# Seven-product stage of a two-layer mixer trunk: running sums in other banks, convolution taps and rotary tables later, SiLU as one activation

## The chip, the cores and the metric

One NeuronCore of a Trainium2 chip runs the whole program in one launch. The metric is the device time of one execution in microseconds, taken as the median of several executions. The profile is one execution, recorded by the hardware.

## What is computed

The reference is a trunk of two layers over 512 tokens of width 1024. Each layer normalises its input and projects it with one wide weight matrix. The columns of the projection feed three groups of heads: a gated linear recurrence (RG-LRU, behind a causal convolution of width 4), a chunked retention with rotary positions, and a spatial gating unit (SGU). Each group is multiplied with a SiLU gate of its own, the results are joined and projected back, and a gated per-layer embedding is added.

```python
y = rms_norm(h, mix_norm[i])
x_lru, g_lru, q, k, v, g_ret, u_sgu, v_sgu, g_sgu = jnp.split(y @ w_in[i], split_points, axis=-1)
lru_out = rg_lru(causal_depthwise_conv(x_lru, ...), ...)     # sigmoid, exp, sqrt, scan
ret_out = retention(q, k, v, positions, ret_norm[i])         # rope on q and k
sgu_out = spatial_gating(u_sgu, v_sgu, ...)                  # LayerNorm of v, then mix
mixed = concatenate([lru_out * silu(g_lru), ret_out * silu(g_ret), sgu_out * silu(g_sgu)])
h = h + mixed @ w_out[i]
h = h + sigmoid(rms_norm(h, ple_norm[i]) @ w_ple_gate[i]) * (p[i] @ w_ple_proj[i])
```

## The kernel before, in words

Every matrix product is made of three TensorE matmuls (`mm3`, lines 217 to 221): each operand is split into a rounded high part and a remainder, and high by high, remainder by high and high by remainder are summed in PSUM. Activations lie transposed, 128 features by 512 tokens. Weights come in chunks of 128 by 1024 through `prefetch`: the load (`emit_raw`), then the split (`emit_cv`), high part on ScalarE (line 173) and remainder on VectorE (line 178). The order of the chunks is written out in `plan`; the split of a chunk is asked for four chunks before its use.

The work is a list of steps. `step` first asks for weights, then issues the step's matmuls, then takes up to three entries of the background queue `bg` (plain functions that issue small work), then the step's eviction, which reads PSUM. Python issues everything in that order, but the order on each engine is settled when the program is built; instructions may pass others that wait.

Of a layer's steps the first ones matter here. The six chunks of the recurrence's input are projected (`feat_steps` with `conv`, lines 531 to 547). `conv` evicts a PSUM bank with one multiplication (line 536), starts the convolution on ScalarE (line 537), adds three taps on VectorE (line 539) and writes the result into `U` by DMAs issued from ScalarE's queue (line 541). Then come seven products (`FAST`, `fast_step`, lines 574 to 606) that replace eight block products of the columns `v` and `v_sgu` after Strassen's scheme; `fast_sums` (lines 494 to 513) forms the sums of activations that five of them need, and is spread over the steps of the convolution by `bg`. Each product is 24 matmuls of 512 columns, two token tiles of 12. They add into three running sums X, Y and Z, each of two PSUM banks. Of the four banks with the tag `mm`, two hold X from the first product (W11) to the last; the other two hold Z for the second product (W21) and then Y for the third (Ta). Z is released by line 593, which adds it to `v`. Four of the seven weight operands are themselves running sums: the tile `rawq` of each half receives W11's block, and further blocks are added onto it in place by DMAs issued from GpSimd's queue (line 148), each one after the split of the sum before it: W11, then Ta, then Tc, then Td.

The order of the products is W11, W21, Ta, Tc, Tb, W22, Td. W22 adds onto Y, which Tb's eviction (lines 597 and 598) has to have read. In layer 0, `bg` holds the nineteen entries of `rope_tables` (lines 406 to 441) during the products. It uses four tiles of the pools with the tags `m2`, `r0` and `r1`. `ln_apply` (the LayerNorm of the SGU) and `bias_rows` are put into `bg` ahead of the last product.

After the products come the SGU's steps: four times a `u` step, whose matmuls end with `mix` (line 698, it reads the normalised `vs`), and a `gs` step, whose eviction is `silu_scaled` (lines 384 to 391); `lru_group` with four short gate steps stands before the second and the fourth pair; `sgu_out`, two more `lru_group` and the six heads of retention follow. The heads need the rotary tables.

Of the kernel before, what the change touches and what calls it, by code (L numbers as in the profile page):

```python
# [10 lines left out]
F32 = mybir.dt.float32  # L11
F32R = mybir.dt.float32r
I32 = mybir.dt.int32
AF = mybir.ActivationFunctionType
ALU = mybir.AluOpType

P = 128
DM, S, DEPTH = 1024, 512, 2
# [8 lines left out]
LRU_GROUPS = [(0, 1), (2, 3), (4, 5), (6, 7)]  # L27


FAST = (("W11", "x11", "X"), ("W21", "x12", "Z"), ("Ta", "u1", "Y"), ("Tc", "v2", "X"), ("Tb", "v3", "X"), ("W22", "u4", "Y"), ("Td", "x22", "X"))  # L30
FIRST = ("W11", "W21", "Ta")
RSQRT_MAGIC = 1597463007.0
ROUND = 12582912.0
# [2 lines left out]
LOOK = 4  # L36
# [58 lines left out]
def trunk(ctx, tc, a):  # L95
# [3 lines left out]
    tp = ctx.enter_context(tc.tile_pool(name="tp", bufs=2))  # L99
    ps = ctx.enter_context(tc.tile_pool(name="ps", bufs=4, space=bass.MemoryType.PSUM))  # L100
    V, SC, G, T = nc.vector, nc.scalar, nc.gpsimd, nc.tensor
# [4 lines left out]
    def slot_tiles(slots, name):  # L106
        return [cp.tile([P, S], F32, tag=f"a{s}", name=f"{name}{i}") for i, s in enumerate(slots)]

    def act_tiles(slots, name):

        t = [cp.tile([P, S], F32R, tag=f"a{s}", name=f"{name}{i}") for i, s in enumerate(slots)]
        return list(zip(t[0::2], t[1::2]))
# [3 lines left out]
    at, offs = 0, {}  # L116
# [77 lines left out]


    bg = deque()
    side = []

    def step(pe, evict=None, look=LOOK, n_bg=3, pre=None):
        prefetch(st["use"] + look)  # L200
        pe()
        for e in side:
            e[0] -= 1
        while side and side[0][0] <= 0:
            side.pop(0)[1]()
        for _ in range(min(n_bg, len(bg))):
            bg.popleft()()
        if pre:
            pre()
        if evict:  # L210
            evict()

    def drain():
        while bg:
            bg.popleft()()
# [7 lines left out]
    def bank(tag="mm", bufs=4, shape=(P, S), name="acc"):  # L223
        return ps.tile(list(shape), F32, tag=tag, name=name, bufs=bufs)
# [54 lines left out]
    nrm = {}  # L279
# [61 lines left out]
        nrm["rn"] = rn  # L341


    def feat_steps(l, y, kinds, evicts, look=LOOK, n_bg=3, mid=None):

        accs = []

        def pe():
            ws = [take(l, *k) for k in kinds]
            for _ in kinds:  # L350
                accs.append(bank())
            for k in range(KD):
                for acc, (wh, wl) in zip(accs, ws):
                    mm3(acc, wh[:, P * k : P * k + P], wl[:, P * k : P * k + P], *y[k], k == 0, k == KD - 1)
            if mid:
                mid()

        step(pe, lambda: [e(acc) for e, acc in zip(evicts, accs)], look=look, n_bg=n_bg)

    def tok_steps(l, y, off, evict):  # L360

# [22 lines left out]
    def silu_scaled(acc, name):  # L384

        x = tp.tile([P, S], F32, tag="sg", name=f"sx{name}", bufs=3)
        V.tensor_mul(x, acc, nrm["R"])
        g = tp.tile([P, S], F32, tag="sgm", name=f"sg{name}", bufs=1)
        SC.activation(g, x, AF.Sigmoid)
        V.tensor_mul(x, x, g)  # L390
        return x


# [10 lines left out]
        return out  # L404

    def rope_tables():
        ang = tp.tile([P, S], F32, tag="m2", name="ang")
        n1 = tp.tile([P, S], F32, tag="r0", name="n1")
        n2 = tp.tile([P, S], F32, tag="r1", name="n2")
        big = 2 * np.pi * 2.0**14  # L410
        c1 = parts(big, 9, 5)
        c2 = parts(2 * np.pi, 9, 5)

        tmp = tp.tile([P, S], F32, tag="m2", name="angt")
        p2 = float(np.float32(2 * np.pi))

        def red(n, c, out=ang, x=ang):
            return lambda: V.scalar_tensor_tensor(out, n, -c, x, op0=ALU.mult, op1=ALU.add)

        def first():  # L420
            V.tensor_copy(ang, posi)
            V.tensor_scalar(ang, ang, inv[:, 0:1], None, op0=ALU.mult)

        def rnd(n, m, x=ang):
            def f():
                V.tensor_scalar(n, x, float(1.0 / m), ROUND, op0=ALU.mult, op1=ALU.add)
                V.tensor_scalar(n, n, -ROUND, None, op0=ALU.add)

            return f

        def last():
            V.tensor_scalar(ang, ang, float(np.float32(3.1415925)), -float(np.float32(3.1415925)), op0=ALU.min, op1=ALU.max)
            SC.activation(sinT, ang, AF.Sin, scale=inv[:, 1:2])
            SC.activation(n1, ang, AF.Abs)
            SC.activation(cosT, n1, AF.Sin, scale=-1.0, bias=cst[:, 0:1])

        ops = [first, rnd(n1, big), red(n1, c1[0]), red(n1, c1[1])]
        ops += [red(n1, c1[2], out=tmp), red(n1, c1[3], out=tmp, x=tmp), rnd(n2, 2 * np.pi, x=tmp), red(n2, c2[0])]
        ops += [red(n1, c1[2]), red(n2, c2[1]), red(n1, c1[3]), red(n2, c2[2]), red(n1, c1[4]), red(n2, c2[3]), red(n2, c2[4])]
        ops += [rnd(n1, 2 * np.pi), red(n1, p2), red(n1, 2 * np.pi - p2), last]  # L440
        return ops
# [25 lines left out]
    y = act_tiles(SLOTS[0]["y"], "y0_")  # L467
# [9 lines left out]
    for l in range(DEPTH):  # L477
# [45 lines left out]
        def blocks(c):  # L523

            at = P * c
            while at < P * c + P:
# [2 lines left out]
                yield b, r, at - P * c, n  # L529
                at += n  # L530

        def conv(c):
            def f(acc):
                u = tp.tile([P, S], F32, tag="r1", name=f"xcv{c}")
                xs = tp.tile([P, S], F32, tag="sg", name=f"xs{c}", bufs=3)
                V.tensor_mul(xs, acc, nrm["R"])  # L536
                SC.activation(u, xs, AF.Identity, scale=col(V_CW, l * 24 + 18 + c), bias=col(V_CB, l * 6 + c))
                for j in range(1, 4):
                    V.scalar_tensor_tensor(u[:, j:], xs[:, : S - j], col(V_CW, l * 24 + 6 * (3 - j) + c), u[:, j:], op0=ALU.mult, op1=ALU.add)  # L539
                for b, r, r0, n in blocks(c):  # L540
                    nc.scalar.dma_start(out=U[r : r + n, b, :], in_=u[r0 : r0 + n, :])
            return f

        feat_steps(l, y, [("in", 0), ("in", P)], [conv(0), conv(1)], mid=norm_finish)
        bg.extend([f for j in range(4) for f in fast_sums(j)])
        for c in range(2, 6):
            feat_steps(l, y, [("in", P * c)], [conv(c)])
            if l == 0 and c == 2:
                softplus()
        rn = nrm["rn"]  # L550
# [10 lines left out]
        vs = slot_tiles(SLOTS[l]["vs"], f"vs{l}_")  # L561
# [8 lines left out]
        banks = {}  # L570

        def fast_step(name, xn, at):

            first = name in FIRST

            def pe():
                ws = [take(l, "fast", (name, c)) for c in range(2)]
                if first:
                    banks[at] = [bank() for _ in range(2)]
                for t in range(2):  # L580
                    for k in range(4):
                        wh, wl = ws[k // 2]
                        c = slice(512 * (k % 2), 512 * (k % 2) + 512)
                        xh, xl = fast_operand(xn, k, t)
                        mm3(banks[at][t], xh, xl, wh[:, c], wl[:, c], first and k == 0, k == 3, more=not first)

            def ev():
                for t in range(2):
                    acc = banks[at][t]
                    if name == "W11":  # L590
                        SC.copy(v4[t], acc)
                    elif name == "W21":
                        V.tensor_add(v4[t], acc, v4[t])  # L593
                    elif name == "Tc":
                        SC.copy(vs[t], acc)
                    elif name == "Tb":
                        SC.copy(vs[2 + t], acc)
                        V.tensor_sub(vs[2 + t], banks["Y"][t], vs[2 + t])
                        ln_stats(2 + t)
                    elif name == "W22":  # L600
                        V.tensor_sub(vs[t], acc, vs[t])
                        ln_stats(t)
                    elif name == "Td":
                        SC.copy(v4[2 + t], acc)

            step(pe, ev, n_bg=3)

        def ln_apply():
            for t in range(4):
                V.bn_aggr(mv[:, t, :], bst[:, t, :, :])  # L610
            vv = tp.tile([P, 4], F32, tag="nv", name="lnv")
            V.tensor_mul(vv, mv[:, :, 1], rn[:, 4:8])
            V.tensor_scalar(vv, vv, EPS, None, op0=ALU.add)
            r = rsqrt(vv, 4)
            V.tensor_mul(r, r, rn[:, 0:4])
            for t in range(4):
                V.tensor_scalar(vs[t], vs[t], mv[:, t, 0:1], r[:, t : t + 1], op0=ALU.subtract, op1=ALU.mult)
# [61 lines left out]
            bg.extend([tanh_exp, sqrts] + [recur(b) for b in grp])  # L679

        drain()
        if l == 0:
            bg.extend(rope_tables())
        for product in FAST[:-1]:
            fast_step(*product)
        bg.extend([ln_apply, bias_rows])
        fast_step(*FAST[-1])
        drain()


        sm = act_tiles(SLOTS[l]["sgu"], f"sm{l}_")
# [65 lines left out]
        sgu_out()  # L757
        drain()
        lru_group(3)
        rm = act_tiles(SLOTS[l]["ret"], f"rm{l}_")  # L760

        def values(h, n):
# [273 lines left out]
```

## Time and profile before

| | |
|---|---|
| median of 3 runs (lowest to highest) | 937.47 us (935.71 to 939.49) |
| the profiled execution's own time | 936.13 us |
| its span | 934.4 us |
| PE (TensorE matmul) busy | 905.3 us, 97% |
| DVE (VectorE) busy | 679.7 us, 73% |
| ACT (ScalarE) busy | 445.2 us, 48% |
| POOL (GpSimd) busy | 61.1 us, 7% |
| mean granted TensorE clock | 0.993 |

PE counts matmuls, PEld weight loads. A matmul is shown from its start to its modelled end, 0.39 us for 512 columns, while the next one starts some 0.23 us after it; a stall is read from the starts. The granted clock is a share of 2.4 GHz; a stretch at 0.5 ran at 1.2 GHz.

### The profile page before, as it was taken

The page shows a single profiled execution, that of the slowest core. Times are in us where ns is not written, and L with a number is a line of the kernel's source. Part 1 is how long each engine was busy: PE and PEld are TensorE (multiplying, and loading weights), DVE is VectorE, ACT ScalarE, POOL GpSimd, SP SyncE. Part 2 cuts the span into 40 slices and gives each one's busy share as a digit, 9 for nine tenths or more (in the row PEclk, how much of TensorE's full clock was granted, in tenths as well). Part 3 has the DMA queues.
Part 4 walks back from the last instruction along what each step waited for, and adds up shares of the span by engine and source line. Part 5 has one row for each costly group of instructions (what it writes and reads, how often), then busy time and mean ns, then how long its engine had stood idle before and what let it go on. Part 6 is the DMA issues. An engine that isn't in the chain of part 4 may idle for free. (4 is left out here: it accounts for less than half of the span.)

```text
span 934.4 us, 11725 instructions
## 1 busy us (share of the span) xinstructions
PE 905.3 (97%) x4354; PEld 751.3 (80%) x4354; DVE 679.7 (73%) x1310; ACT 445.2 (48%) x650; POOL 61.1 (7%) x57
## 2 busy tenths in 40 slices
PE   8969999999999999999999899999999999999997
PEld 5747887788898888888877688877889888888886
DVE  7998798897757784456649788889786767534564
ACT  6644566853232343343556446767333334434353
POOL 3210000000000000110321100000000000011020
PEclk9999999999999999999999999999999999999999
DMA  8876422332223233342586843222322324333302
GB/s 288 220 167 166 130 78 78 107 98 90 71 87 100 83 117 101 112 142 68 138 180 142 183 137 91 79 90 91 113 68 68 108 73 113 96 102 118 113 1 90
DMA packets 35034, 105.14 MB, mean 113 GB/s; under 512 B 4641, under 2 KB 5665, under 8 KB 34977
## 3 DMA queue, kind: packets, MB, share of 16 engines
q1 hardware_dynamic: 27536, 85.42, 28.6%
q0 software_dynamic: 3456, 12.58, 7.5%
q10 hardware_dynamic: 3984, 6.38, 2.3%
q8 instruction: 34, 0.56, 0.2%
q14 instruction: 24, 0.19, 0.1%
HBM read 95.99 MB, written 2.10 MB: 105 GB/s over the span
## 5 line engine op out<-in xcount | busy, mean ns | idle before, releaser
L173 ACT CAST whi<-raw 128x1024 fp32r<-128x1024 f32 (+2 forms) x158 | 154.3, 978 | 285.6 <-PE acc L220 210.4
L219 PE MATMUL acc<-y,whi 128*128 128x512 f32 x608 | 241.6, 397 | 0.5 <-DVE whi L171 0.4
L220 PE MATMUL acc<-y,whi 128*128 128x512 f32 x608 | 237.5, 391 | 2.5 <-DVE y L286 2.4
L221 PE MATMUL acc<-y,wlo 128*128 128x512 f32 x608 | 237.8, 391 | 1.0 <-DMA wlo<-in_wall 0.6
L178 DVE TENSOR_TENSOR wlo<-raw,whi 128x1024 fp32r<-128x1024 f32 (+3 forms) x154 | 172.6, 1123 | 77.9 <-ACT whi L173 77.3
L220 PEld LDWEIGHTS acc<-y,whi 128*128 128x128 f32 x608 | 114.4, 188 | 27.0 <-DVE y L286 4.5
L221 PEld LDWEIGHTS acc<-y,wlo 128*128 128x128 f32 x608 | 114.1, 188 | 26.3 <-DVE wlo L178 1.3
L219 PEld LDWEIGHTS acc<-y,whi 128*128 128x128 f32 x608 | 114.3, 188 | 24.0 <-DVE whi L171 0.6
L302 POOL TENSOR_TENSOR nacc<-nacc,sq 128x512 f32<-128x512 f32 (+1 forms) x26 | 36.5, 1403 | 496.2 <-ACT sq L292 495.9
L219 PE MATMUL acc<-z,whi 128*128 128x512 f32 (+1 forms) x144 | 53.0, 368 | 0.0
L221 PE MATMUL acc<-z,wlo 128*128 128x512 f32 (+1 forms) x144 | 52.8, 366 | 0.0
L220 PE MATMUL acc<-z,whi 128*128 128x512 f32 (+1 forms) x144 | 52.7, 366 | 0.0
L220 PE MATMUL acc<-wlo,y 128*128 128x256 f32 (+1 forms) x112 | 37.5, 335 | 2.8 <-DVE wlo L178 2.8
L219 PE MATMUL acc<-whi,y 128*128 128x256 f32 (+1 forms) x112 | 37.3, 334 | 1.8 <-DVE xs L536 1.8
L219 PE MATMUL acc<-whi,uy 128*128 128x512 f32 x64 | 27.5, 429 | 10.4 <-DVE v L593 8.1
L221 PE MATMUL acc<-rm,wlo 128*128 128x512 f32 x96 | 37.4, 389 | 0.0
L219 PE MATMUL acc<-ml,whi 128*128 128x512 f32 x96 | 37.4, 389 | 0.0
L220 PE MATMUL acc<-ml,whi 128*128 128x512 f32 x96 | 37.3, 389 | 0.0
L219 PE MATMUL acc<-rm,whi 128*128 128x512 f32 x96 | 37.3, 389 | 0.0
L220 PE MATMUL acc<-rm,whi 128*128 128x512 f32 x96 | 37.3, 389 | 0.0
L221 PE MATMUL acc<-ml,wlo 128*128 128x512 f32 x96 | 37.3, 389 | 0.0
L221 PE MATMUL acc<-whi,y 128*128 128x256 f32 (+1 forms) x112 | 36.8, 329 | 0.0
(236 smaller groups left out, 1640.6 us busy)
## 6 DMA issues: line engine op xcount, KB each, us to landing
raw<-in_wall SPq DMA_DIRECT2D x120, 512.0 KB, 3.5
raw<-in_wall SPq DMA_DIRECT2D x32, 384.0 KB, 3.0
rawq<-in_wall POOLq DMA_DIRECT2D x12, 512.0 KB, 5.5
wlo<-in_wall POOLq DMA_DIRECT2D x8, 512.0 KB, 8.6
hT<-in_xT SPq DMA_DIRECT2D x8, 256.0 KB, 5.9
rawq<-in_wall SPq DMA_DIRECT2D x4, 512.0 KB, 6.1
raw<-in_wall POOLq DMA_DIRECT2D x4, 512.0 KB, 7.2
out_dram<-o SPq DMA_DIRECT2D x8, 256.0 KB, 2.1
```

The source lines that it names most:

```text
L173: SC.copy(hi[:m, c], r[:m, c])
L178: V.tensor_sub(lo[:m, c], r[:m, c], f32(hi[:m, c]))
L219: T.matmul(out, wh, xh, start=first, stop=False, skip_group_check=more)
L220: T.matmul(out, wh, xl, start=False, stop=False, skip_group_check=more)
L221: T.matmul(out, wl, xh, start=False, stop=last, skip_group_check=more)
L302: (V if d == KD - 1 else G).tensor_add(nrm["acc"][:, c], nrm["acc"][:, c], sq[:, :n])
```

## The change

The order of the last two products is exchanged: Td now precedes W22. Z takes the two banks with the tag `sc` in place of two of the four `mm` banks. A second queue, `lazy`, gives one entry per step after those of `bg`. `conv` now multiplies the evicted bank into a tile that stays (`xs_at`), and puts the rest (start, three taps, DMAs) into `lazy`; the steps of chunks 2 to 5 take nothing from it, so that the six entries go with the first six products. `rope_tables` uses four long-lived tiles and goes into `lazy` after the seven products of layer 0; what is left of it is issued before the heads. `ln_apply` is issued directly after the seven products, `bias_rows` before them. `silu_scaled` calls one Silu activation in place of a Sigmoid and a multiplication.

```diff
-FAST = (("W11", "x11", "X"), ("W21", "x12", "Z"), ("Ta", "u1", "Y"), ("Tc", "v2", "X"), ("Tb", "v3", "X"), ("W22", "u4", "Y"), ("Td", "x22", "X"))
+FAST = (("W11", "x11", "X"), ("W21", "x12", "Z"), ("Ta", "u1", "Y"), ("Tc", "v2", "X"), ("Tb", "v3", "X"), ("Td", "x22", "X"), ("W22", "u4", "Y"))
...
-    def step(pe, evict=None, look=LOOK, n_bg=3, pre=None):
+    def step(pe, evict=None, look=LOOK, n_bg=3, pre=None, n_lazy=1):
...
+        for _ in range(min(n_lazy, len(lazy))):
+            lazy.popleft()()
...
         V.tensor_mul(x, acc, nrm["R"])
-        g = tp.tile([P, S], F32, tag="sgm", name=f"sg{name}", bufs=1)
-        SC.activation(g, x, AF.Sigmoid)
-        V.tensor_mul(x, x, g)
+        SC.activation(x, x, AF.Silu)
...
-        ang = tp.tile([P, S], F32, tag="m2", name="ang")
-        n1 = tp.tile([P, S], F32, tag="r0", name="n1")
-        n2 = tp.tile([P, S], F32, tag="r1", name="n2")
+        ang, n1, n2, tmp = slot_tiles((20, 21, 30, 31), "rope")
...
-        tmp = tp.tile([P, S], F32, tag="m2", name="angt")
...
+        xs_at = slot_tiles([*SLOTS[l]["vs"], *SLOTS[l]["v"][2:]], f"xs{l}_")
+
         def conv(c):
-            def f(acc):
+            xs = xs_at[c]
+
+            def taps():
                 u = tp.tile([P, S], F32, tag="r1", name=f"xcv{c}")
-                xs = tp.tile([P, S], F32, tag="sg", name=f"xs{c}", bufs=3)
-                V.tensor_mul(xs, acc, nrm["R"])
                 SC.activation(u, xs, AF.Identity, ...)
                 for j in range(1, 4):
                     V.scalar_tensor_tensor(u[:, j:], xs[:, : S - j], ...)
                 for b, r, r0, n in blocks(c):
                     nc.scalar.dma_start(out=U[r : r + n, b, :], in_=u[r0 : r0 + n, :])
+
+            def f(acc):
+                V.tensor_mul(xs, acc, nrm["R"])
+                lazy.append(taps)
...
-            feat_steps(l, y, [("in", P * c)], [conv(c)])
+            feat_steps(l, y, [("in", P * c)], [conv(c)], n_lazy=0)
...
-                    banks[at] = [bank() for _ in range(2)]
+                    banks[at] = [bank("sc", 2) if at == "Z" else bank() for _ in range(2)]
...
+        bg.append(bias_rows)
+        for product in FAST:
+            fast_step(*product)
+        ln_apply()
         if l == 0:
-            bg.extend(rope_tables())
-        for product in FAST[:-1]:
-            fast_step(*product)
-        bg.extend([ln_apply, bias_rows])
-        fast_step(*FAST[-1])
-        drain()
+            lazy.extend(rope_tables())
...
         lru_group(3)
+        while lazy:
+            lazy.popleft()()
```

## Rows read from the trace of the kernel before

**Rows 1.** The page, part 1: busy time of each engine.

```profile
PE 905.3 (97%) x4354; PEld 751.3 (80%) x4354; DVE 679.7 (73%) x1310; ACT 445.2 (48%) x650; POOL 61.1 (7%) x57
```

**Rows 2.** Stretches: length, busy us per engine, granted clock, DMA share, GB/s.

```profile
46.80:100.30 53.50, 43.99 (x171) 33.81 (x170) 49.81 (x86) 24.85 (x33) 4.32 (x5) 0.94 0.67 163
504.80:551.80 47.00, 41.49 (x170) 32.32 (x169) 39.81 (x69) 25.25 (x33) 4.31 (x5) 0.96 0.62 151
...
67.30:71.00 3.70, 3.70 (x10) 2.93 (x11) 2.50 (x5) 0.43 (x1) 0.03 (x1) 0.55 1.03 188
...
87.70:91.20 3.50, 3.48 (x8) 2.82 (x9) 3.50 (x6) 0.00 (x0) 0.00 (x0) 0.51 0.47 149
...
523.30:528.00 4.70, 4.70 (x14) 3.70 (x15) 2.24 (x6) 1.04 (x1) 0.00 (x0) 0.64 1.04 214
...
100.30:165.00 64.70, 64.11 (x298) 52.36 (x297) 54.20 (x89) 42.17 (x57) 0.00 (x0) 1.00 0.29 88
...
112.00:125.00 13.00, 13.00 (x63) 10.50 (x62) 9.76 (x15) 12.82 (x17) 0.00 (x0) 1.00 0.29 82
```

**Rows 3.** Timeline of PE, layer 0: start, us, instruction, idle before and its releaser.

```profile
53.16 1.02 PE L621 MATMUL rs<-ws,ones 128*128 128x512 f32 x2
...
67.29 0.76 PE L219 MATMUL acc<-whi,uy 128*128 128x512 f32 x1 [5.04 <-DVE v L593]
...
84.83 0.39 PE L220 MATMUL acc<-wlo,uy 128*128 128x512 f32 x1
85.06 0.39 PE L221 MATMUL acc<-whi,uy 128*128 128x512 f32 x1
87.72 0.80 PE L219 MATMUL acc<-whi,uy 128*128 128x512 f32 x1 [2.27 <-DVE vs L598]
```

**Rows 4.** Waits of PE, whole span: us in total, times, longest.

```profile
PE acc L219 <- DVE v L593: 8.1, 2, 5.0
PE acc L220 <- DVE wlo L178: 2.8, 4, 1.3
...
PE acc L219 <- DVE xs L536: 1.8, 3, 0.8
```

**Rows 5.** Timeline of DVE, layer 0, while PE waits for the third product.

```profile
62.26 0.73 DVE L539 SCALAR_TENSOR_TENSOR xcv<-xs,vec,xcv 128x509 f32<-128x509 f32 x1
...
64.39 0.41 DVE L427 TENSOR_SCALAR n<-n 128x512 f32<-128x512 f32 x1
64.73 1.21 DVE L178 TENSOR_TENSOR wlo<-rawq,whi 128x1024 fp32r<-128x1024 f32 x1
...
66.47 0.67 DVE L593 TENSOR_TENSOR v<-acc,v 128x512 f32<-128x512 f32 x1
```

**Rows 6.** Timelines of POOL, ACT and DVE: the next sum of the same weight tile.

```profile
66.46 0.86 POOL L148 DMA_DIRECT2D rawq<-in_wall  x1 [0.61 <-issue]
...
73.11 1.05 ACT L173 CAST whi<-rawq 128x1024 fp32r<-128x1024 f32 x1 [1.49 <-DMA rawq<-in_wall]
...
74.19 1.23 DVE L178 TENSOR_TENSOR wlo<-rawq,whi 128x1024 fp32r<-128x1024 f32 x1 [1.32 <-ACT whi L173]
```

**Rows 7.** Groups of DVE instructions by line and form: busy us, mean ns, idle before.

```profile
L418 DVE SCALAR_TENSOR_TENSOR ang<-n,ang 128x512 f32<-128x512 f32 x12 | 8.2, 681 | 0.1
L390 DVE TENSOR_TENSOR sxr<-sxr,sgr 128x512 f32<-128x512 f32 x12 | 8.2, 681 | 0.0
```

**Rows 8.** Timeline of ACT around the first group of recurrence gates, layer 0.

```profile
115.03 0.62 ACT L389 ACTIVATE sgs<-sxs 128x512 f32<-128x512 f32 x1
...
120.08 1.28 ACT L661 ACT_TABLE_LOAD   x1
121.38 1.34 ACT L661 ACTIVATE rg<-rg,spm 96x512 f32<-96x512 f32 x2
```

**Rows 9.** Timeline of DVE, layer 1: LayerNorm after the sixth product (W22).

```profile
547.96 0.68 DVE L601 TENSOR_TENSOR vs<-acc,vs 128x512 f32<-128x512 f32 x1
...
553.63 1.92 DVE L617 TENSOR_SCALAR vs<-vs,mv,rs_y 128x512 f32<-128x512 f32 x4
```

More of the change, by code (lines that the diff above doesn't have):

```diff
@@ L196, in trunk @@
     bg = deque()
+    lazy = deque()
     side = []
-    def step(pe, evict=None, look=LOOK, n_bg=3, pre=None):
+    def step(pe, evict=None, look=LOOK, n_bg=3, pre=None, n_lazy=1):
         prefetch(st["use"] + look)
@@ L341, in norm_bcast, with feat_steps @@
         nrm["rn"] = rn
-    def feat_steps(l, y, kinds, evicts, look=LOOK, n_bg=3, mid=None):
+    def feat_steps(l, y, kinds, evicts, look=LOOK, n_bg=3, mid=None, n_lazy=1):
         accs = []
@@ L356, in pe @@
                 mid()
-        step(pe, lambda: [e(acc) for e, acc in zip(evicts, accs)], look=look, n_bg=n_bg)
+        step(pe, lambda: [e(acc) for e, acc in zip(evicts, accs)], look=look, n_bg=n_bg, n_lazy=n_lazy)
     def tok_steps(l, y, off, evict):
@@ L604, in ev @@
                         SC.copy(v4[2 + t], acc)
-            step(pe, ev, n_bg=3)
+            step(pe, ev)
         def ln_apply():
```

## The prediction

> **What bounds the kernel now.** I read the engines' shares first. TensorE is busy for 97% of the span [rows 1], so apart from a shorter matmul stream, which this change does not bring, only its stalls and its slow clock can be won. The waits of TensorE name what it stalls on: VectorE, and above all line 593 and the splits of weights [rows 4]. The stretches then say where: the seven products take 53.50 us in layer 0 and 47.00 in layer 1 [rows 2]. What would they take without a stall? Two matmuls start 0.23 us apart [rows 3]; seven products of 24 matmuls are 168, so 38.6 us, and the product for `bias_rows` adds 1.0 [rows 3]: 39.6. Layer 0 thus loses 13.9 us and layer 1 7.4, together 21.3. That is the most that this stage can give.
>
> The timeline shows two kinds of loss. The third product (Ta) waits 5.04 us in layer 0 for line 593, and the sixth (W22) 2.27 us for line 598 [rows 3]; line 593 costs 8.1 us in two waits [rows 4], so 3.1 in layer 1. Behind each wait the clock is low: 0.55, 0.51 and 0.64 of 2.4 GHz over 3.70, 3.50 and 4.70 us [rows 2], so partly or wholly at 1.2 GHz after TensorE had stood still. Each costs its length times the missing share: 1.7 us three times.
>
> VectorE is why the waits are long. It is busy 49.81 of the 53.50 us [rows 2], and in the wait itself it does a convolution tap (62.26), a rotary operation (64.39) and the split of Ta's own second weight half (64.73) before line 593 at 66.47 [rows 5].
>
> **The change, part by part.**
>
> *Banks of Z.* Y gets free banks, since the convolution's banks that it takes over are long read. Line 593 no longer stands before Ta: 5.04 + 1.7 in layer 0, 3.1 + 1.7 in layer 1, 11.5 in all. A condition is that Ta's weights are there, and its split ended only at 65.9 [rows 5], 3.7 us after W21's last matmul. So the bank alone would win little; the relief of VectorE has to come with it.
>
> *Taps and rotary tables.* All 18 taps of layer 0, some 0.73 us each [rows 5], were issued ahead of Ta; now some two stages of three are due before it. The rotary tables leave altogether: 14 operations of 0.68 us [rows 7] and nine of some 0.41 [rows 5], 13.2 us. So VectorE is ahead by over 10 us where Ta's split is due, and that split's input was ready earlier. I take the whole 11.5. The waits for splits and banks inside the first two products are 2.8 + 1.8 [rows 4]; with the stumbles after them they are what is left of the 21.3, that is 5.8 after the 4.0 of the next part. Of these I take half, 2.9: a split also waits for its load.
>
> *Td before W22.* W22 no longer follows the eviction of Tb that it needs; 24 matmuls, 5.5 us, lie between, and the wait was 2.3. That gives 2.27 + 1.7 = 4.0, in layer 0 alone. Td adds onto X, whose copy by ScalarE has 12 matmuls of cover, as for Tb before. Td's loads on POOL's queue move up too, but they start when Tc's split ends, as now; W22's, on SP's, follow without need.
>
> *What the taps do in their new place.* They and their DMAs sit on ScalarE's queue between the copies that free X; a DMA waiting there for a tap holds up those copies and the splits. VectorE's load in layer 0's products becomes 49.8 - 13.2 + 6.4 (the nine taps that ran ahead of the stage, at 0.71) = 43.0 against 39.6. The cost lies between 0 and 3.4; 1.5, since the sums of activations move ahead in turn. If that cover fails, the copy of X is late next.
>
> *LayerNorm.* `ln_apply` was covered by Td. Now only the first `u` step lies between W22 and `mix`. In layer 1 it ran from 547.96 to 555.55, 7.6 us from the last subtraction [rows 9], against 5.5 us of matmuls. The shortfall is 2.1 per layer, or nothing if the gate's matmuls pass `mix`, as the product for `bias_rows` passed others (line 621 ran at 53.16, in the second product, though it is asked for with the seventh) [rows 3]. I take 1.0 each, 2.0, between 0 and 4.2.
>
> *Rotary tables in the SGU stage of layer 0.* VectorE has 10.5 us idle there (64.70 - 54.20) [rows 2]. It gets 13.2 and loses four gate multiplications of 0.68 [rows 7]: 10.5 net, so the idle is used up. TensorE's loss lies between 0 and 10.5. In that stage it loses 0.6 at a VectorE load of 84%, in the products of layer 0 13.9 at 93% [rows 2]. But the weights are split four chunks ahead, and the rotary operations wait for nobody: 3.0.
>
> *Silu.* The 32 multiplications (22 us) go from VectorE where TensorE does not wait for it; worth nothing by themselves. No row has a Silu. If it shares Sigmoid's table the cost is nothing; if not, loads are added at 1.28 us each [rows 8]. Between 0 and 18 (see the fourth rival); I take 1.0, since ScalarE is busy for 48% [rows 1] and its splits run ahead.
>
> The load's row is followed by its activation 1.30 us later, 120.08 to 121.38 [rows 8]. The Trainium skill (ScalarE: Activation LUTs, What ACT_TABLE_LOAD costs) counts 1283 ns and a drain of some 1380 ns for every switch. By that figure fourteen more switches would be an estimated 37 us of ScalarE rather than 18; the trace shows the first part alone.
>
> **Sum.** 11.5 + 4.0 + 2.9 = 18.4 won; 1.5 + 2.0 + 3.0 + 1.0 = 7.5 spent; 10.9 less. From the profiled execution's 936.13 that is 925.2 us. The median of the runs is 1.3 above that execution, the lowest 0.4 below it, within what I can't resolve. With all 21.3 won and nothing spent it is 914.8; with the two big terms won and 3.4 + 4.2 + 3.0 + 1.0 spent 932.2.
>
> **The rivals.**
>
> *The chain of sums becomes the bound* (0.14). One link, from the end of Ta's split (65.94) over POOL's load at 66.46 and the cast at 73.11 to the end of the next split at 75.42, takes 9.5 us [rows 5, 6], and Ta and Tc lie one product (5.5) apart. If Ta's split is just in time, Tc waits 4.0 in each layer: 933.2. For it: the link is a load, which no relief of VectorE shortens. Against it: W11's split is due four chunks ahead and stood in VectorE's queue.
>
> *The rotary tables fall on the path* (0.08). All 10.5 in place of 3.0: 932.7. For it: no idle is left there. Against it: the heads, which use them, come much later.
>
> *The build undoes the order* (0.07). As engines' orders are settled at the build, taps may be placed ahead of the splits again; then only the price of a part moves and it stays near 936.
>
> *The tables of ScalarE* (0.11), the case on the slower side. Tanh follows Sigmoid without a load, Exp and Sqrt take one each (120.08 is Exp's) [rows 8]. If Silu needs a load of its own, the two layers have nine changes more between it and Sigmoid; four groups of gates have a SiLU among their Sigmoids (115.03) [rows 8], one change more each; and the tables' Sin one: 14 loads, 18 us. ScalarE is full around these groups, 12.82 of 13.00 us [rows 2]. If the 18 are on the path in place of 1.0, it is 942.1. It decides once the splits queued behind the loads are later than their four chunks of lead. A rule beside it: the Trainium skill (ScalarE: Activation LUTs, Rules for kernel authors) asks to group by table set and finish one before the next, which speaks against this part; no run here shows yet which set Silu is in.
>
> **How the numbers follow.** The forecast itself has 0.60. A measurement of this kernel can tell about 0.5%, 4.7 us. Faster by more than that: nearly all of the forecast (0.59), half of the chain (0.07), half of the rotary case (0.04), 0.70. Slower: the tables, 0.11. Between: the rest, 0.19. The range goes from 914, everything won, to 936, the build's case; it leaves out the slower rival and some of the edge.
>
> **What would show it.** Right: no line 593 among TensorE's waits, the first product to the last in some 42 us per layer, granted clock near 1 there, W22 without a wait; in layer 0's SGU stage VectorE near full and waits of TensorE of a few us. The chain would show as Tc waiting for `wlo` of `rawq`; the tables as more ACT_TABLE_LOAD rows and TensorE waiting for splits behind them; LayerNorm as a wait of `mix` or none. I am wrong if the products stay above 46 us, or if the SGU stage grows by more than 6.

## The result, and the profile after

The changed kernel takes 927.41 us (median of 4 runs, 927.21 to 927.96); the kernel before, run beside it, took 937.24 (935.71 to 939.49). The ratio is 0.9894, with an interval of 0.9873 to 0.9915: faster by 1.1%. The forecast was 925.2. The profiled execution took 927.45 us, 8.7 less than that of before, with a span of 925.7.

The engines first, as in [rows 1]; this is part 1 of the page of the changed kernel.

```profile
PE 903.4 (98%) x4354; PEld 750.0 (81%) x4354; DVE 663.4 (72%) x1278; ACT 460.9 (50%) x663; POOL 59.7 (6%) x57
```

VectorE has 32 instructions less, the multiplications of the gates; ScalarE has 13 more. The stretches tell more: the products of layer 0, those of layer 1, as much of layer 0's SGU stage as [rows 2] show, and then two stretches right behind stalls of TensorE (columns as in [rows 2]).

```profile
47.08:90.67 43.59, 41.25 (x172) 32.89 (x171) 38.43 (x60) 23.09 (x30) 3.45 (x4) 0.96 0.81 206
496.82:541.68 44.86, 41.20 (x172) 32.89 (x170) 36.13 (x53) 22.31 (x28) 3.45 (x4) 0.96 0.64 159
90.67:155.40 64.73, 64.15 (x296) 52.10 (x295) 61.45 (x107) 47.89 (x59) 0.00 (x0) 1.00 0.27 86
...
75.30:80.00 4.70, 4.70 (x14) 3.70 (x15) 3.78 (x6) 2.48 (x4) 0.00 (x0) 0.64 0.79 253
526.32:530.00 3.68, 3.68 (x10) 2.90 (x11) 3.01 (x5) 2.43 (x3) 0.00 (x0) 0.58 0.33 71
```

Read by one rule in both traces, from the first matmul of W11 to the first of the first `u` step (the stretches of [rows 2] end a little earlier), the products went from 53.53 to 43.59 us in layer 0 and from 47.40 to 44.86 in layer 1: 12.5 won. From there to the first transpose of the first head, the SGU stage with its gates went from 103.45 to 104.55 and from 103.43 to 104.97: 2.6 given back. The rest of the difference of 8.7 lies in shifts of 0.3 to 0.6 elsewhere. In these 64.73 us of layer 0's SGU stage VectorE is now busy for 61.45 (it was 54.20) and TensorE for 64.15 (it was 64.11 of 64.70): the rotary tables went in without more idle time of TensorE.

What TensorE waits for, whole span:

```profile
PE acc L222 <- ACT vs L600: 5.6, 3, 3.4
...
PE acc L223 <- DVE xc L484: 1.3, 4, 0.3
...
PE mx L702 <- DVE vs L622: 0.4, 1, 0.4
```

The wait for the first eviction of Z (line 593 of before, now 598) is gone, and so is W22's for Tb. In their place a new wait heads the list, which no row of before shows: line 600, ScalarE's copy of X after Tc. Its two large cases in the timeline of TensorE:

```profile
75.29 0.50 PE L222 MATMUL acc<-whi,uy 128*128 128x512 f32 x1 [1.92 <-ACT vs L600]
...
526.32 0.50 PE L222 MATMUL acc<-whi,uy 128*128 128x512 f32 x1 [3.42 <-ACT vs L600]
```

Behind both the granted clock is low (the last two stretches above: 0.64 over 4.70 us, 0.58 over 3.68), so partly at 1.2 GHz. That costs 4.70 x 0.36 + 3.68 x 0.42 = 3.2 us more, so that this one wait costs 8.8. Why is the copy late? The timeline of ScalarE around the two, with the DMA issues that they go back to:

```profile
67.93 1.39 ACTq L541 DMA_DIRECT2D U<-xcv  x2
...
73.96 0.81 ACT L537 ACTIVATE xcv<-xs,vec 128x512 f32<-128x512 f32 x1 [1.83 <-DMA U<-xcv]
...
74.68 0.56 ACT L600 COPY vs<-acc 128x512 f32<-128x512 f32 x1
...
515.98 1.18 ACTq L541 DMA_DIRECT2D U<-xcv  x2
...
524.99 0.81 ACT L537 ACTIVATE xcv<-xs,vec 128x512 f32<-128x512 f32 x1 [3.68 <-DMA U<-xcv]
...
525.71 0.56 ACT L600 COPY vs<-acc 128x512 f32<-128x512 f32 x1
```

Line 537 starts the convolution of a chunk in the tile `xcv`, which has two buffers. A buffer is free once the DMAs that carry it into `U` have landed. The entry at 73.96 needs the buffer whose DMAs were issued from 67.93 on, and starts 4.6 us after the last issue ended; the one at 524.99 starts 7.8 us after the end of the issues from 515.98 on. The DMA engines were busy for 0.99 and 0.92 of these two stretches, so the landings were long where the engines were nearly full. ScalarE stands idle for 1.83 and 3.68 us with the copy of X behind it. My theory after this: the late taps won the time and the tile's two buffers gave much of it back; the banks, the order, the rotary tables and Silu are each to be tried.

### The profile page after: what moved, and what is told of

Read it like the earlier page. It is cut to its first block, busy times and chain, and to the rows that moved or that the text cites. A ratio compares the mean times of both kernels' runs of the same rounds, so it can differ in the third digit from the quotient of the medians.

```text
span 925.7 us, 11717 instructions
## 1 busy us (share of the span) xinstructions
PE 903.4 (98%) x4354; PEld 750.0 (81%) x4354; DVE 663.4 (72%) x1278; ACT 460.9 (50%) x663; POOL 59.7 (6%) x57
## 4 chain that ended last, share of the span: by engine, by line
PE 78%; DVE 6%; DMA 6%; ACT 5%; issue 3%; POOL 1%; SPq 0%; ACTq 0%; DVEq 0%; POOLq 0%
PE acc L223 23%; PE acc L224 23%; PE acc L222 23%; DMA rawq<-in_wall 2%; DVE wlo L178 2%; DMA U<-xcv 1%; PE sc L811 1%; PE o L834 1%; DMA raw<-in_wall 1%; ACT whi L173 1%; DMA wlo<-in_wall 1%; PE o L836 1%; PE kv L822 1%; DVE U L680 1%; POOL nacc L305 1%
## 5 line engine op out<-in xcount | busy, mean ns | idle before, releaser
L899 DVE TENSOR_TENSOR hT<-hT,acc 128x512 f32<-128x512 f32 x16 | 11.0, 687 | 29.9 <-PE acc L224 29.9
```

The lines of the kernel that those rows point to most:

```text
L899: V.tensor_add(hT[:, d, :], hT[:, d, :], accs[j])
```

## The experiments

All figures are medians, with the ratio to runs of the kernel before on the same chip. "Products" are the two stages measured as above, layer 0 and layer 1, in one profiled execution each. The kernel before took 935.43 to 937.24 us in the runs beside these kernels, so two kernels are compared by their ratios; a difference of medians alone is good to some 1.8 us.

| kernel | us | ratio, interval | products |
|---|---|---|---|
| changed kernel | 927.41 | 0.9894 (0.9873 to 0.9915) | 43.59 + 44.86 |
| e1_banks_only | 933.21 | 0.9966 (0.9951 to 0.9981) | 48.83 + 47.66 |
| e2_old_banks | 927.76 | 0.9914 (0.9890 to 0.9939) | 43.48 + 43.63 |
| e3_sigmoid | 928.96 | 0.9931 (0.9907 to 0.9955) | 44.30 + 44.66 |
| e4_taps_after_evict | 925.39 | 0.9880 (0.9853 to 0.9908) | 43.25 + 41.89 |
| e5_four_tiles | 921.71 | 0.9845 (0.9816 to 0.9875) | 39.41 + 42.64 |
| e6_rope_early | 926.30 | 0.9908 (0.9880 to 0.9935) | 42.47 + 42.36 |
| e7_four_tiles_sigmoid | 920.83 | 0.9845 (0.9824 to 0.9866) | 39.46 + 43.24 |
| e8_four_after_evict | 919.93 | 0.9832 (0.9805 to 0.9858) | 39.00 + 38.98 |
| e9_old_order | 931.15 | 0.9942 (0.9921 to 0.9964) | 47.70 + 46.74 |
| e10_taps_only | 928.01 | 0.9920 (0.9897 to 0.9943) | 45.70 + 45.02 |
| e11_four_old_banks | 922.30 | 0.9853 (0.9832 to 0.9873) | 39.22 + 42.82 |
| e12_four_old_order | 921.55 | 0.9846 (0.9824 to 0.9868) | 41.01 + 40.66 |

### The banks: alone, and taken out

e1 is the kernel before with Z's new banks alone; e2 is the changed kernel with the old banks.

```diff
-                    banks[at] = [bank() for _ in range(2)]
+                    banks[at] = [bank("sc", 2) if at == "Z" else bank() for _ in range(2)]
```

> The kernel before with one edit: Z takes the two banks tagged sc. Theory (relief of VectorE and the banks work together, the relief being the larger part): line 593 no longer stands before Ta, but Ta then waits for the split of its own weights, which in the trace of before ended at 65.9 us (layer 0) and 521.9 (layer 1) while W21 ended at 62.2 and 520.1. So Ta starts 1 to 2 us sooner per layer: 933 to 936 us, with TensorE waiting for wlo (line 178) in place of line 593. Rival A (the banks are the whole gain): 927 to 929. Rival B (the banks are worth nothing): 937.

> The changed kernel with Z back on the mm banks, all else kept. Theory (relief is the larger part): in the changed kernel line 598 (v plus Z) ran at 57.3 and 59.5 us while Ta started at 58.9, so with VectorE relieved the old banks cost little: Ta's second tile waits a little, 927.5 to 930 us. Rival A (the banks are the whole gain): 936 to 938, with a wait for line 598 of 3 us or more in each layer.

Alone, the banks won 0.34%. The waits of TensorE in e1:

```profile
PE acc L220 <- DVE wlo L178: 6.9, 8, 2.3
PE acc L219 <- ACT whi L173: 4.3, 4, 2.0
```

Line 593 is gone, and 11.2 us of waits for splits of weights stand in its place, where before had 2.8 for `wlo` [rows 4]. In e2 the old banks are back, no product waits for line 598, and the ratio lies within the interval of the changed kernel. So the banks win a little where the taps are early, and nothing that could be measured where they are late.

### The new wait: the place of the taps, and four tiles

e4 issues an entry of `lazy` behind the evictions of a step instead of ahead of them. e5 leaves that and gives `xcv` four buffers: the tile takes the tags `r1` and `r0` in turn.

```diff
-        for _ in range(min(n_lazy, len(lazy))):
-            lazy.popleft()()
         if pre:
             pre()
         if evict:
             evict()
+        for _ in range(min(n_lazy, len(lazy))):
+            lazy.popleft()()
```

```diff
-                u = tp.tile([P, S], F32, tag="r1", name=f"xcv{c}")
+                u = tp.tile([P, S], F32, tag=f"r{1 - c % 2}", name=f"xcv{c}")
```

> The changed kernel with the entry of the lazy queue issued after the step's eviction in place of before it. Theory (Tb's second tile waits for the copy of X, line 600, because that copy stands on ScalarE behind line 537, which waits for the DMA into U to release the tile xcv): the copies come ahead, the waits of 1.92 us (layer 0) and 3.42 us (layer 1) and the slow clock behind them (some 1.5 us each) go, 920 to 923 us. Rival (the copy is late because ScalarE is full of splits): the waits stay, 926 to 928.

> The changed kernel with the convolution's tiles xcv taken in turn from the tags r0 and r1, so that four exist in place of two; the order of the queue entries is kept. Theory (line 537 waits for the DMA of the tile two entries back): with four tiles that wait is gone although line 537 still stands before the copy of X, so 920 to 923 us and no wait for line 600. Rival (the place in ScalarE's queue alone matters, behind the DMAs that wait for taps): 925 to 928, waits for line 600 remain.

e4's median is 2.0 us below the changed kernel's, between what theory and rival had named, and the intervals overlap; waits of 2.3 us for line 600 and 0.9 for line 602 stayed. e5's is 5.7 below (4.6 by the ratios; the two intervals just touch), and the two longest waits in its products and right behind them are these:

```profile
PE mx L702 <- DVE vs L622: 1.7, 2, 1.3
PE acc L222 <- ACT vs L602: 1.3, 1, 1.3
```

No wait for line 600. Nothing but the count of buffers was changed, so the wait was the tile's. What else is left in the products are 1.4 us for a split inside Tc in layer 1. The clock follows: the mean granted clock of the executions is 0.996 to 0.999, against 0.994 to 0.996. The waits of `mix` for the LayerNorm are now 1.7 where the changed kernel had 0.4. Why is not shown: e2 has 1.0 of it in layer 0 with products as long as the changed kernel's (43.48 us).

### Silu or Sigmoid

e3 is the changed kernel, e7 is e5, with the Sigmoid and the multiplication back.

```diff
-        SC.activation(x, x, AF.Silu)
+        g = tp.tile([P, S], F32, tag="sgm", name=f"sg{name}", bufs=1)
+        SC.activation(g, x, AF.Sigmoid)
+        V.tensor_mul(x, x, g)
```

> The changed kernel with Sigmoid and a multiplication in place of Silu, all else kept. The SGU stage (first u step to the first head) grew from 103.45 to 104.55 us in layer 0 and from 103.43 to 104.97 in layer 1. Theory (the 13 more table loads are that growth): loads fall from 40 to 27 or 28, layer 1's stage goes back to 103.5, 924.5 to 926 us. Rival (LayerNorm behind the seven products is the growth): layer 1's stage stays at 105, 927 to 929 us. Second rival (the multiplication saved counts for TensorE): above 929.

> Four tiles for the convolution (as e5_four_tiles, 921.7 us) and Sigmoid with a multiplication in place of Silu. Theory (table loads are the growth of the SGU stage): 918.5 to 920 us, SGU stages of 104 to 104.5 and 103.5. Rival (LayerNorm is): 921 to 923 us.

The groups of table loads on ScalarE in the changed kernel (busy us and mean ns behind the bar):

```profile
L649 ACT ACT_TABLE_LOAD x11 | 14.1, 1283 | 2.7 <-DVE U L680 2.6
L391 ACT ACT_TABLE_LOAD x10 | 12.8, 1283 | 0.2
L666 ACT ACT_TABLE_LOAD x8 | 10.3, 1283 | 0.1
L671 ACT ACT_TABLE_LOAD x8 | 10.3, 1283 | 0.1
L939 ACT ACT_TABLE_LOAD x2 | 2.6, 1283 | 0.0
L233 ACT ACT_TABLE_LOAD x1 | 1.3, 1283 | 1.3 <-PEq L1034 1.3
```

That is 40, where the kernel before has 27; in e3 it is 27 plus two for Sin. The two groups that differ most, in e3 (its lines stand two lower from 393 on):

```profile
L392 ACT ACT_TABLE_LOAD x6 | 7.7, 1283 | 0.1
L651 ACT ACT_TABLE_LOAD x4 | 5.1, 1283 | 1.7 <-DVE U L682 1.6
```

So Silu does need a load of its own beside Sigmoid. What the loads cost can be seen in layer 1, where no rotary tables are in the way: from the products to the first head 104.97 us with Silu and 104.07 with Sigmoid, and with four tiles 105.01 and 104.08. That is 0.9 twice. In layer 0, where the rotary tables run in the same stage, the kernels with Silu are 0.5 and 0.3 shorter. The whole time tells nothing: e7 stands to before as e5 does (0.9845 both), and e3's interval overlaps that of the changed kernel. Both kernels took longer than the theory had named (928.96 and 920.83 us), and layer 1's stage went back to 104.07 and not to 103.5, so the loads are only a part of that stage's growth; the wait of `mix`, 0.4 us in layer 1 of both, is another. In e3 the copy of X came late as well (its line 602: 5.9 us in three waits).

### The rotary tables back among the products

e6 is the changed kernel with `rope_tables` in `bg` during the products, and in its old tiles.

```diff
-        ang, n1, n2, tmp = slot_tiles((20, 21, 30, 31), "rope")
+        ang = tp.tile([P, S], F32, tag="m2", name="ang")
...
+        if l == 0:
+            bg.extend(rope_tables())
         bg.append(bias_rows)
...
-        if l == 0:
-            lazy.extend(rope_tables())
```

> The changed kernel with the rotary tables back in the background queue during the seven products of layer 0, in the old tiles. Theory (the relief of VectorE in layer 0 is made of the taps and of the rotary tables in like parts): the products of layer 0 grow from 43.6 us to 47 to 50, the SGU stage of layer 0 shrinks by 0.3 to 1, 930 to 933 us. Rival (the taps alone are the relief, as in layer 1, which has no rotary tables): 926.5 to 928.5 us.

My theory named too much: 926.30 us, no slower than the changed kernel. The stage of layer 0 in e6:

```profile
47.51:89.98 42.47, 40.09 (x172) 31.68 (x170) 40.42 (x62) 22.21 (x29) 3.46 (x4) 1.00 0.77 187
```

VectorE is busy 40.42 of 42.47 us, a larger share than before the change (49.81 of 53.50 [rows 2]), and the stage is 11 us shorter. So how full VectorE is does not set the stage; that it is what stands in its queue ahead of a split or an eviction fits e10 below, but is argued here. Nor did the SGU stage get shorter without the tables: 105.80 against 104.55. A part of that is a wait of 0.86 us for a split on VectorE at 91.92, right behind the products.

### The order of Td and W22

e9 is the changed kernel with W22 ahead of Td.

```diff
-FAST = (("W11", "x11", "X"), ("W21", "x12", "Z"), ("Ta", "u1", "Y"), ("Tc", "v2", "X"), ("Tb", "v3", "X"), ("Td", "x22", "X"), ("W22", "u4", "Y"))
+FAST = (("W11", "x11", "X"), ("W21", "x12", "Z"), ("Ta", "u1", "Y"), ("Tc", "v2", "X"), ("Tb", "v3", "X"), ("W22", "u4", "Y"), ("Td", "x22", "X"))
```

> The changed kernel with W22 before Td again. Theory (W22 has to wait for Tb's eviction from Y): a wait of W22 for line 603 of some 2 us in layer 0 and slow clock behind it, 1.7 us: 930 to 932 us. Rival (with VectorE relieved that eviction is in time, and Td's weights come later anyway): 926.5 to 929 us.

Its median is 3.7 us above the changed kernel's (4.5 by the ratios), with intervals that do not touch, and both layers lost (4.1 and 1.9 us of products). But W22's own wait for Tb's eviction was 1.03 us in layer 0 and none in layer 1. The longest waits were these, with one row of ScalarE behind them:

```profile
PE acc L222 <- ACT vs L600: 6.3, 2, 4.4
PE acc L222 <- ACT whi L173: 2.4, 2, 1.6
...
PE acc L223 <- DVE wlo L178: 1.5, 2, 0.8
...
60.39 1.04 ACT L173 CAST whi<-rawq 128x1024 fp32r<-128x1024 f32 x1 [5.27 <-DMA rawq<-in_wall]
```

The copy of X costs only 0.7 us more than in the changed kernel (6.3 against 5.6). What grew most are the waits for splits, 3.9 us, all in layer 0 inside Ta and Tc, which come ahead of the exchanged pair; the changed kernel has 0.42 there. These splits waited for the loads of their weights. In layer 1 the clock after the copy's wait is lower (0.93 over the products, against 0.96). So most of what e9 lost lies elsewhere than in the order's own wait, and why the loads landed later was not tried. e12 asks what is left of the order with four buffers.

### The taps alone, and four tiles with one part undone

e10 is the kernel before with the late taps and nothing else. The others start from e5: e8 issues the taps behind the evictions (as e4), e11 has the old banks, e12 the old order.

```diff
+    lazy = deque()
...
+        for _ in range(min(n_lazy, len(lazy))):
+            lazy.popleft()()
...
+        xs_at = slot_tiles([*SLOTS[l]["vs"], *SLOTS[l]["v"][2:]], f"xs{l}_")
...
+                V.tensor_mul(xs, acc, nrm["R"])
+                lazy.append(taps)
```

> The kernel before with the late convolution taps alone: Z on its old banks, W22 ahead of Td, rotary tables among the products, Sigmoid. Theory (the taps alone are the relief of VectorE; banks, rotary tables and Silu were worth nothing once it is there, and the order is worth about 3.7 us): 930 to 932 us, no product waits for the first eviction's line, and the waits that remain are W22's for Tb's eviction and the copy of X behind the entry of a tap tile. Rival (the parts work only together): 934 to 936 us, with the wait of the bank still there.

> The changed kernel with four buffers for the tap tile and the taps issued after the evictions of a step instead of ahead of them. Theory (the 1.3 us left at the copies of a step are the taps queued ahead of them): 919 to 921 us and no wait for a copy in the products. Rival (what is left lies elsewhere): 921.5 to 923 us.

> The changed kernel with four buffers for the tap tile and Z back on the banks that X uses. Theory (with VectorE relieved the bank is free in time): 921 to 923 us and no product waits for the first eviction's line. Rival (the wait for the bank comes to light once the copy's wait is gone): 924 to 927 us, with that line back among the waits.

> The changed kernel with four buffers for the tap tile and W22 ahead of Td as before. Theory (W22 waits for Tb's eviction by itself): 924 to 926 us, with waits of W22's products for the line that makes Tb. Rival (the order was worth its 3.7 us only through the copy of X that came late): 921 to 923 us and no such wait.

e10 came out at 928.01, below what theory and rival gave: one part of the change makes 0.80% of its 1.06%, and the intervals of the two overlap. Its products, 90.7 us, have 10.2 of the 12.5 that the whole change won. The bank's wait is gone there with Z on its old banks. What TensorE waits for in e10's stage, layer 0 and layer 1 (line 608 is Tb's eviction, line 605 the copy of X):

```profile
60.90 0.95 PE L222 MATMUL acc<-whi,uy 128*128 128x512 f32 x3 [2.02 <-ACT whi L173]
...
80.37 0.80 PE L222 MATMUL acc<-whi,uy 128*128 128x512 f32 x1 [2.35 <-DVE vs L608]
...
521.67 0.50 PE L222 MATMUL acc<-whi,uy 128*128 128x512 f32 x1 [1.58 <-ACT vs L605]
...
532.82 0.50 PE L222 MATMUL acc<-whi,uy 128*128 128x512 f32 x1 [2.69 <-DVE vs L608]
```

And ScalarE in layer 1, where the start of a tap entry (line 542 there) waits 3.35 us for its tile as in the changed kernel. It stands behind the copies of X and the first copy of Tb (line 607), but ahead of the second, which line 608 needs:

```profile
523.41 0.59 ACT L605 COPY vs<-acc 128x512 f32<-128x512 f32 x1 [0.32 <-DVE xc L489]
...
524.85 0.58 ACT L607 COPY vs<-acc 128x512 f32<-128x512 f32 x1
528.78 0.82 ACT L542 ACTIVATE xcv<-xs,vec 128x512 f32<-128x512 f32 x1 [3.35 <-DMA U<-xcv]
530.44 0.57 ACT L607 COPY vs<-acc 128x512 f32<-128x512 f32 x1
```

The wait for the tile is the same and TensorE sees it here too, by another way: Tb's last matmul started at 527.02, its second copy ran only at 530.44, line 608 at 532.08, and W22's second token tile, which had to wait for it, started at 532.82. The wait for line 605 at 521.67 also goes back to an entry of line 542, which stood at 519.60 ahead of the copy. So the position that the build gives to that one instruction decides which product pays for its wait. In e9 the same entry stands at 529.90, ahead of a copy of X at 530.62, and Tb pays 4.4. e9 and e10, both in the old order with two buffers, differ by 3.1 us (2.1 by the ratios, whose intervals overlap); what makes it was not tried.

e12 equals e5 (921.55 and 921.71, ratios 0.9846 and 0.9845). In its timeline W22 waits once, 1.30 us in layer 0; the row of layer 1 below is a wait for a split, not for Tb:

```profile
77.80 0.50 PE L222 MATMUL acc<-whi,uy 128*128 128x512 f32 x1 [1.30 <-DVE vs L603]
...
515.05 0.50 PE L222 MATMUL acc<-whi,uy 128*128 128x512 f32 x1 [0.35 <-ACT whi L173]
```

The rival's time holds, though not its "no such wait": the order is worth nothing that could be measured beside four buffers. e11, with the old banks, takes 922.30, within what was expected of worthless banks. e8 is the fastest of all, 919.93, 1.7% below the kernel before, with an interval that lies below that of the changed kernel; those of e8 and e5 overlap. Its two stages of products:

```profile
47.09:86.09 39.00, 39.00 (x172) 31.88 (x170) 37.09 (x57) 21.17 (x28) 3.45 (x4) 1.00 0.90 221
493.28:532.26 38.98, 38.98 (x171) 31.92 (x170) 35.57 (x54) 21.05 (x27) 3.46 (x4) 1.00 0.71 175
```

39.0 us in each layer, the granted clock 1.00, VectorE at 95% in layer 0. The timeline of TensorE shows no wait in the products of either layer; the waits of `mix` for the LayerNorm, 1.24 us in layer 0 and 0.40 in layer 1, come behind them. This is the stage's floor: 78.0 us where the kernel before took 100.9 and the changed one 88.5.

## Why the prediction was right, and which of its steps were not

The time was 2.2 us from the forecast and the sign was right, but the closeness came of two errors that partly cancelled. On the forecast's own account the products were to shrink by 18.4 - 1.5 = 16.9 and shrank by 12.5; the rest was to cost 6.0 and cost, with the shifts elsewhere, 3.8. So the time was right in part by luck. By the prediction's own signs the products came out above the 42 us per layer that were named, though below the 46 that would have refuted it, and their granted clock was 0.96 and not near 1.

- **What can be won at most.** Said 21.3 against 39.6 per layer; e8 shows a floor of 39.0, so 22.9. Right.
- **"Banks of Z", 11.5.** The waits behind it did go, but not by the banks. e10 loses them without the banks, e2 and e11 have the old banks and none of the waits; the banks alone are worth 0.34% and trade the wait for others. The sentence "the bank alone would win little; the relief of VectorE has to come with it" was half right: the relief does it by itself.
- **"Taps and rotary tables".** I counted two reliefs. e6 shows that the rotary tables were none: back among the products they cost nothing that can be measured, at a VectorE share of 95%. The failed step is that VectorE "is ahead by over 10 us" by its load; what counted were the taps ahead of Ta's split and of line 593 [rows 5], as e10 shows, which moves the taps alone. The tables alone were not tried late.
- **"Td before W22", 4.0 in layer 0 alone.** e9 gives 3.7 in sum, but spread over both layers and mostly through splits that waited for their loads; W22's own wait was 1.03. e12 gives none with four buffers. The size agreed by luck, the mechanism only in a small part.
- **Half of what is left, 2.9.** A little undersized. The changed kernel's products lie 10.5 above the floor, and 8.8 of that is the new wait; so at most 1.7 of the old losses stayed, where I had left 2.9.
- **"What the taps do in their new place", 1.5, between 0 and 3.4.** This is the mis-sized term: 8.8 us by the sum of stalls and slow clock, 6.4 of products by the difference to e5 (88.4 against 82.0), 4.6 of the whole time by the ratios (in e5 layer 0's SGU stage is 1.4 longer). The upper bound came from VectorE's load, which was the wrong row. The mechanism named was close, ScalarE's queue with the copy of X late next; but what stands there is not a DMA that waits for a tap. It is the tap's first instruction, waiting for its tile until an earlier DMA has landed. I had counted the DMAs as issues and not as what holds a buffer. [rows 6] had shown, for a load of weights, how far issue and landing lie apart.
- **"LayerNorm", 2.0.** 0.4 in the changed kernel, 1.7 in e5. The exception named happened in layer 0: the 24 matmuls of the first `gs` step and the twelve of the first recurrence gates ran ahead of `mix`, until 104.33. In layer 1 only one of `gs` did.
- **"Rotary tables in the SGU stage", 3.0.** Nothing there: TensorE idles 0.58 us of that stretch, as before, and e6, without them, has the longer stage. The rival by the rotary tables falls too.
- **"Silu", 1.0, and the rival of ScalarE's tables.** The count was right, 13 more loads where 14 were guessed. The price, 1.0 for both layers, came out at 0.9 in layer 1's stage and below nothing in layer 0's, though the loads are 16.7 us of ScalarE. The rival fell; that the splits behind the loads ran ahead enough is argued.
- **The chain of sums.** Its wait shows as 0.42 us inside Tc in layer 0, where 4.0 were named: the rival fell.

The Trainium skill (ScalarE: Activation LUTs, What ACT_TABLE_LOAD costs) has 1283 ns and a drain of some 1380 for each switch. The timeline of ScalarE at the first group of gates of layer 0, where Silu stands among the Sigmoids, agrees with the first and shows none of the second: each activation starts 1.29 to 1.30 us after the start of its load.

```profile
102.59 1.28 ACT L649 ACT_TABLE_LOAD   x1
103.88 0.69 ACT L649 ACTIVATE rg<-acc,vec 96x512 f32<-96x512 f32 x1
104.58 1.28 ACT L391 ACT_TABLE_LOAD   x1
105.88 0.64 ACT L391 ACTIVATE sxs<-sxs 128x512 f32<-128x512 f32 x1
106.53 1.28 ACT L649 ACT_TABLE_LOAD   x1
107.83 1.83 ACT L649 ACTIVATE rg<-acc,vec 96x512 f32<-96x512 f32 x3
```

The rule of the Trainium skill (ScalarE: Activation LUTs, Rules for kernel authors) to finish one table set before the next is broken here. It costs a measured 0.9 us in that stage of layer 1. The waits of TensorE that the kernels with Silu have more of are for remainders made by VectorE: `xc`, 1.3 us in four waits, where before had 0.5 in two and e3 has 0.9 in three.

**What stays open.** Why the SGU stage of layer 0 is 0.5 to 2.8 us longer in all kernels with the late taps (103.99 to 106.24) than before (103.45) is only partly told. The waits of `mix` there are none to 1.35 us of it; the longer waits for `xc` and for the casts of `sm` are another part, also in e7 with its Sigmoids. Why those come is open. So is why the loads of weights landed later in e9. Nor was it tried whether Z's banks, Silu and the rotary tables could all be left out of e8.

## What to carry to other kernels

Work that is moved to a later place takes its buffers along: count for each moved instruction when its tile comes free, the landing of the DMA that reads it included, and who stands behind it on its engine. A busy share near 95% is no bottleneck by itself; look for what stands in the queue ahead of the instruction that the critical engine waits for. And when a change has several parts that take away the same wait, a part can be worth something alone and nothing beside another, as Z's banks were: run each alone and each taken out before one is credited.

## What the runs showed that was not expected

Silu took loads of its own beside Sigmoid, 10 at line 391, and 11 of Sigmoid's at line 649 where e3 has 4. But Sin after a Silu took none in the changed kernel; in e3 the two Sin activations took one load each. The landing of small DMAs decided more than their size would say: the two that carry one 128x512 tile into `U` held its buffer for 4.6 and 7.8 us after their issue, while the DMA engines were busy for 0.99 and 0.92.

And a stall's length did not tell whether the clock fell behind it. In e2 the copy of X came 3.21 us late in layer 0 and 2.56 in layer 1; the clock behind the longer wait was full, behind the shorter one 0.65 (columns as in [rows 2]):

```profile
76.77:81.40 4.63, 4.63 (x20) 3.86 (x21) 3.70 (x6) 3.97 (x5) 0.00 (x0) 1.00 0.61 196
525.79:530.40 4.61, 4.61 (x14) 3.66 (x15) 3.95 (x7) 2.51 (x4) 0.00 (x0) 0.65 0.26 57
```

So the 1.7 us that the prediction put on each stall is a price read from three of them, not one that every stall pays.
